# A hybrid decoder trunk on one core: the time-step weights as 64 columns side by side, and two row tiles' norm statistics moved to ScalarE

## The chip, the core and the metric

The kernel runs on one core of one Trainium2 chip. The core has five engines that matter here, each with an instruction stream of its own that runs in order: TensorE (PE in the profile, with its weight loads shown apart as PEld), VectorE (DVE), ScalarE (ACT), GpSimd (POOL) and SyncE (SP, which only issues DMAs). Semaphores tie the streams together. The metric is the device time of one execution in microseconds (us), given as the median of a few runs. TensorE was granted its full clock throughout (0.998 of it over the execution that was profiled).

## What is computed

The input is a residual stream `x` of 1024 positions by 1024 channels, in float32. It is normalised row by row, and then one layer follows: a wide projection whose columns feed a Conformer convolution branch and a Mamba-2 state-space branch, their gated sum, a second norm, and a causal convolution FFN with a third norm. Cut to what the change touches:

```python
def layer_norm(x, g, b):
    mu = jnp.mean(xf, axis=-1, keepdims=True)
    var = jnp.mean(jnp.square(xf - mu), axis=-1, keepdims=True)
    return (xf - mu) * lax.rsqrt(var + LN_EPS) * g + b
...
h = layer_norm(x, ln_in_g, ln_in_b)
u = h @ w_in[l]          # ... | ssm x,B,C | ssm dt (32 columns) | ...
...
dt = jax.nn.softplus(dt_raw + dt_bias)     # time steps, one for each of 32 heads
a_head = -jnp.exp(a_log)
```

The 32 columns `dt_raw` of the projection give the time steps, one for each position and head. They set the decays of the state-space branch.

## The kernel before, in words

**Precision.** A projection keeps float32 accuracy by splitting both factors in two parts, a rounded high part (`hi`, type fp32r) and the remainder (`lo`). Each product is then three matmuls: hi*hi, hi*lo and lo*hi (`mm3`, L164 to L169). For a weight tile of 128x1024 (eight blocks of 128x128, one for each group of 128 input channels), `weights` (L150) loads it into a buffer `st_...` by DMA, ScalarE copies the high part to `w_...` (L155), and VectorE, or GpSimd where it is told so, subtracts to get the low part (L156). There are three buffers for loads and three for split weights. A new weight tile's copy on ScalarE must wait until TensorE is done with the tile three before it.

**Halves.** The 1024 positions go in two halves of 512. A half has four row tiles of 128 positions. `ln_in` (L235) loads the four tiles `x_0` to `x_3`, normalises each, stores it for later, and transposes it by TensorE into `hT`, again as hi and lo.

**The input norm of a tile** (before): VectorE takes the statistics of two halves of the row (L208) and merges them to mean and variance (L222); ScalarE takes a square root (L223) and VectorE the reciprocal (L224); VectorE then applies it in two passes over the 128x1024 tile, in place: subtract the mean and multiply by the gain (L228), multiply by the reciprocal and add the bias (L231). TensorE transposes the tile in eight 128x128 blocks, four to a PSUM bank (L193); for each bank ScalarE copies the high part out (L199) and VectorE subtracts to get the low part (L200). There are four such PSUM banks (`sm_...`), so the banks of `x_2` are those that `x_0` used.

**The first columns** (`first_columns`, L349): three column tiles of the projection come first in each half, the time-step tile `w_c_40` (32 real columns, filled up with zeros to 128), one tile of B (`w_c_32`) and one of C (`w_c_36`). Each is multiplied with `hT` in two steps of 256 positions, so that the first step needs only `x_0` and `x_1`: for each tile and step, 3 products times 8 blocks = 24 matmuls of 128x256 (L358). That makes 144 matmuls a half. In the first half GpSimd subtracts the low parts of these three weight tiles, in the second VectorE does. After them come the columns of x, in matmuls of 128x512 (L167 to L169).

**The time steps** (`time_steps`, L262): ScalarE adds the bias to the 32 rows of the finished `dt` product (L265, `dtc`), TensorE transposes it in four pieces of 32x128 (L270), and a chain of small VectorE and ScalarE operations follows.

**What sets the order.** The program is written in loops, and a scheduler that plays through a timeline of its own orders the instructions of each engine, with the priorities given in the code (`tc.high_priority`). The order of each engine is fixed when the kernel is built. `x_0` and `x_1` have a higher priority than `x_2` and `x_3`. On TensorE the matmuls of the first columns and the transposes of `x_2` and `x_3` are woven into one another.

## Time and profile before

| | us |
|---|---|
| median of 3 runs | 2008.04 (2006.31 to 2008.36) |
| the execution that was profiled | 2007.04 |
| its span, first instruction to last | 2005.2 |
| TensorE busy in the span | 1971.1 (98%), 9164 matmul records |
| VectorE busy | 1693.9 (84%) |
| ScalarE busy | 1022.5 (51%) |
| GpSimd busy | 178.0 (9%) |

A timeline row gives the start, the length of the group, the engine, the line, the operation, output and inputs, shape, and how many instructions the group holds; square brackets name the idle time ahead of it and what ended it. Instructions on one engine overlap a little at their ends, and a matmul's shown length includes its way through the array, so distances between starts are what count there. In a row of the windows, each engine has its busy time and, in brackets, the number of its instructions in the window. In a group that is asked for by its line, three numbers give the shortest, the median and the longest duration in ns. The row of waits names who waited for what, the total, how often, and the longest.

### The profile page before, as it was taken

What the parts mean: (1) busy time and instruction counts of PE and PEld (TensorE: products, weight loads), DVE (VectorE), ACT (ScalarE), POOL (GpSimd) and SP (SyncE); (2) the same over time, 40 slices, a digit from 0 to 9 for tenths busy, and PEclk for the clock granted to TensorE, in tenths of its full rate; (3) what the DMA queues carried; (4) which work ended last, traced back from release to release, by engine and by line L of the source; (5) the groups of instructions that cost most, each with busy time, mean ns of one, the idle gap of its engine ahead of it and who ended that gap; (6) DMA issues with size and microseconds to landing.
All of it is one profiled execution on the core that took longest, in us unless ns stands there. A gap on an engine that the chain in (4) does not pass through costs nothing. (4 is left out here: it accounts for less than half of the span.)

```text
span 2005.2 us, 24594 instructions
## 1 busy us (share of the span) xinstructions
PE 1971.1 (98%) x9164; PEld 1620.4 (81%) x9164; DVE 1693.9 (84%) x2261; ACT 1022.5 (51%) x1480; POOL 178.0 (9%) x144
## 2 busy tenths in 40 slices
PE   7999999999999999999999999999999999999998
PEld 6888888888888888888888888877778888888886
DVE  7599999979865868999998977578998878778768
ACT  4465654556453265665545546255554444553432
POOL 2010101001300000100000122001000000011000
PEclk9999999999999999999999999999999999999999
DMA  6223223233445532222323253487442232368573
GB/s 222 88 70 95 79 87 123 85 111 106 168 128 183 221 109 74 84 90 85 115 90 111 100 173 121 131 283 250 146 158 104 100 121 95 106 217 266 184 241 110
DMA packets 97031, 272.20 MB, mean 136 GB/s; under 512 B 11216, under 2 KB 11216, under 8 KB 96912
## 3 DMA queue, kind: packets, MB, share of 16 engines
q1 hardware_dynamic: 88992, 246.78, 37.2%
q0 software_dynamic: 5616, 19.66, 2.7%
q10 hardware_dynamic: 2304, 4.20, 0.6%
q8 instruction: 72, 1.18, 0.3%
q14 instruction: 47, 0.39, 0.1%
HBM read 221.05 MB, written 49.55 MB: 135 GB/s over the span
## 5 line engine op out<-in xcount | busy, mean ns | idle before, releaser
L421 DVE SCALAR_TENSOR_TENSOR c<-v,pc,c 128x512 f32<-128x512 f32 x480 | 374.5, 803 | 6.4 <-ACT c L410 5.0
L479 POOL TENSOR_TENSOR au<-seg_mv,head_of 128x1024 fp32r<-128x1024 f32 x32 | 77.0, 2408 | 958.5 <-PE sm L488 728.2
L167 PE MATMUL acc<-hT,w_c 128*128 128x512 f32 x352 | 141.1, 401 | 0.0
L168 PE MATMUL acc<-hT,w_c 128*128 128x512 f32 x352 | 140.7, 400 | 0.0
L169 PE MATMUL acc<-hT,w_c 128*128 128x512 f32 x352 | 138.5, 393 | 0.0
L910 DVE SCALAR_TENSOR_TENSOR fo<-u,pc,fo 128x1024 f32<-128x1024 f32 x88 | 111.4, 1285 | 0.4 <-ACT fo L906 0.4
L376 DVE SCALAR_TENSOR_TENSOR xbc<-u,pc,xbc 128x512 f32<-128x512 f32 x144 | 109.6, 773 | 0.7 <-ACT xbc L374 0.5
L167 PE MATMUL acc<-h1s,w_s 128*128 128x512 f32 x264 | 104.5, 396 | 2.3 <-ACT u L894 2.3
L169 PE MATMUL acc<-h1s,w_s 128*128 128x512 f32 x264 | 104.0, 394 | 0.0
L168 PE MATMUL acc<-h1s,w_s 128*128 128x512 f32 x264 | 103.5, 392 | 0.0
L167 PE MATMUL acc<-w_z,hT 128*128 128x512 f32 x256 | 100.9, 401 | 0.0
L168 PE MATMUL acc<-w_z,hT 128*128 128x512 f32 x256 | 100.9, 394 | 0.0
L169 PE MATMUL acc<-w_z,hT 128*128 128x512 f32 x256 | 100.7, 396 | 0.0
L155 ACT CAST w_c<-st_c 128x1024 fp32r<-128x1024 f32 x50 | 52.6, 1052 | 88.9 <-PE acc L169 68.1
L1049 ACT CAST w_dn<-dr 128x1024 fp32r<-128x1024 f32 (+1 forms) x73 | 60.8, 842 | 71.9 <-DVE dr L979 31.1
L1050 DVE TENSOR_TENSOR w_dn<-dr,w_dn 128x1024 fp32r<-128x1024 f32 (+1 forms) x73 | 70.1, 967 | 14.8 <-ACT w_dn L1049 14.6
L168 PEld LDWEIGHTS acc<-hT,w_c 128*128 128x128 f32 x352 | 66.1, 188 | 17.0 <-issue 3.8
L169 PEld LDWEIGHTS acc<-hT,w_c 128*128 128x128 f32 x352 | 66.1, 188 | 16.2 <-issue 2.6
L167 PEld LDWEIGHTS acc<-hT,w_c 128*128 128x128 f32 x352 | 66.1, 188 | 16.0 <-issue 2.6
L156 DVE TENSOR_TENSOR w_c<-st_c,w_c 128x1024 fp32r<-128x1024 f32 x47 | 60.5, 1288 | 20.2 <-ACT w_c L155 20.2
L167 PE MATMUL sm<-h1b,w_s 128*128 128x512 f32 x176 | 69.6, 396 | 0.0
L169 PE MATMUL sm<-h1b,w_s 128*128 128x512 f32 x176 | 69.3, 394 | 0.0
(354 smaller groups left out, 5703.1 us busy)
## 6 DMA issues: line engine op xcount, KB each, us to landing
st_c<-wcol SPq DMA_DIRECT2D x50, 512.0 KB, 3.5
st_z<-wz SPq DMA_DIRECT2D x32, 512.0 KB, 3.5
st_wo<-wo SPq DMA_DIRECT2D x24, 512.0 KB, 4.0
ra<-wup SPq DMA_DIRECT2D x22, 512.0 KB, 3.5
rb<-wup SPq DMA_DIRECT2D x22, 512.0 KB, 3.4
t_scr<-fo POOLq DMA_DIRECT2D x22, 512.0 KB, 3.4
dr<-t_scr SPq DMA_DIRECT2D x44, 256.0 KB, 4.0
dr<-wdown SPq DMA_DIRECT2D x38, 256.0 KB, 4.3
```

Of the source, the lines that this page charges most:

```text
L155: A.copy(w[:, 0, :], st)
L156: (eng or V).tensor_tensor(out=w[:, 1, :], in0=st, in1=w[:, 0, :].bitcast(F32), op=ALU.subtract)
L167: TE.matmul(ps, wa(0), xa(0), start=start, stop=False, skip_group_check=more)
L168: TE.matmul(ps, wa(0), xa(1), start=False, stop=False, skip_group_check=more)
L169: TE.matmul(ps, wa(1), xa(0), start=False, stop=stop, skip_group_check=more)
L376: V.scalar_tensor_tensor(out=o, in0=u[:, k : k + HALF], scalar=pc[:, wc + k : wc + k + 1], in1=o, op0=ALU.mult, op1=ALU.add,)
L421: V.scalar_tensor_tensor(out=accs[i], in0=v[:, k : k + HALF], scalar=pc[:, wc + k : wc + k + 1], in1=accs[i], op0=ALU.mult, op1=ALU.add,)
L479: G.tensor_tensor(out=au, in0=seg_mv[:, c, :].unsqueeze(1).to_broadcast([P, 8, P]), in1=head_of[:, g, :].unsqueeze(2).to_broadcast([P, 8, P]),
L910: V.scalar_tensor_tensor(out=o, in0=u[:, k : k + T], scalar=pc[:, wc + k : wc + k + 1], in1=o, op0=ALU.mult, op1=ALU.add,)
L1049: A.copy(w[:, 0, cs], src)
L1050: V.tensor_tensor(out=w[:, 1, cs], in0=src, in1=w[:, 0, cs].bitcast(F32), op=ALU.subtract)
```

## The change

It has two parts.

**The time-step weights.** The tile of 128 columns, of which 32 are real, is replaced by 64 columns for each block: the 32 high parts and, beside them, the 32 low parts (`weights_side_by_side`). Only the real columns are split, 128x256 elements in place of 128x1024, by ScalarE and VectorE in both halves of the positions (GpSimd has no part in it any more). One matmul with these 64 columns gives hi*h and lo*h at once, in 64 rows of the output. With the high and the low part of `hT` that is 2 x 8 = 16 matmuls of 64x256 for each step of 256 positions in place of 24. The bias is added to 64 rows (it is zero in the second 32), and the four transposes become four float32 matmuls with a 64x32 matrix `fold`, two identities on top of each other, which add the two groups of rows while they transpose. (The product then holds lo*lo as well.)

**The statistics.** For `x_2` and `x_3` of the first half alone, `ln_stats_act` takes the place of the VectorE statistics: ScalarE passes over the tile once to sum it, multiplies the sum by -1/1024, passes over it a second time to sum the squares of what is left after the mean, and takes the square root with the factor 1/1024. VectorE still takes the reciprocal and applies the norm. The second pass reads the tile that VectorE's first step then overwrites.

```diff
+    fold = statep.tile([2 * HEADS, HEADS], F32, name="fold")
+    V.tensor_add(fold, ident[: 2 * HEADS, :HEADS], ident[: 2 * HEADS, HEADS : 2 * HEADS])
...
+    def weights_side_by_side(src, name):
+        with tc.high_priority(offset=4000):
+            st = wst.tile([P, D], F32, tag="st", name=f"st_{name}")
+            SY.dma_start(st, src)
+            w = wsp.tile([P, 2, D], F32R, tag="w", name=f"w_{name}")
+            sv = st.rearrange("p (k c) -> p k c", k=KD)[:, :, :HEADS]
+            wv = w[:, 0, : KD * 2 * HEADS].rearrange("p (k c) -> p k c", k=KD)
+            hi, lo = wv[:, :, :HEADS], wv[:, :, HEADS:]
+            A.copy(hi, sv)
+            V.tensor_tensor(out=lo, in0=sv, in1=hi.bitcast(F32), op=ALU.subtract)
+        return wv
...
+    def ln_stats_act(pl, t, name):
+        work = pl.tile([P, D], F32, tag="ln_work", name=f"work_{name}")
+        mv = pl.tile([P, 1, 2], F32, tag="ln_mv", bufs=2, name=f"mv_{name}")
+        rs = pl.tile([P, 1], F32, tag="ln_rs", bufs=2, name=f"rs_{name}")
+        mean, var = mv[:, 0, 0:1], mv[:, 0, 1:2]
+        A.activation(out=work, in_=t, func=AF.Identity, accum_out=var)
+        A.mul(mean, var, -1.0 / D)
+        A.activation(out=work, in_=t, func=AF.Square, bias=mean, accum_out=var)
+        A.activation(out=rs, in_=var, func=AF.Sqrt, bias=eps, scale=1.0 / D)
+        V.reciprocal(out=rs, in_=rs)
+        return mv, rs
...
-                    mv, rs = ln_stats(pl, [xt], f"in{hh}_{t}")
-                    ln_apply(xt, mv, rs, 0, *gb)
+                    if first and t >= 2:
+                        mv, rs = ln_stats_act(pl, xt, f"in{hh}_{t}")
+                        ln_apply(xt, mv, rs, 0, *gb, op=ALU.add)
+                    else:
+                        mv, rs = ln_stats(pl, [xt], f"in{hh}_{t}")
+                        ln_apply(xt, mv, rs, 0, *gb)
...
-        dtc = pl.tile([HEADS, HALF], F32, tag="yo", name=f"dtc{hh}")
+        n2 = 2 * HEADS
+        dtc = pl.tile([n2, HALF], F32, tag="yo", name=f"dtc{hh}")
...
-            TE.transpose(
+            TE.matmul(
                 pt[:, c * HEADS : (c + 1) * HEADS],
                 dtc[:, c * P : (c + 1) * P],
-                ident[:HEADS, :HEADS],
+                fold,
+                start=True,
+                stop=True,
             )
...
-        ws = [weights(wcol[ct], f"c{hh}_{ct}", eng=None if hh else G) for ct in cts]
+        wd = weights_side_by_side(wcol[cts[0]], f"c{hh}_{cts[0]}")
+        ws = [weights(wcol[ct], f"c{hh}_{ct}", eng=None if hh else G) for ct in cts[1:]]
         pss = [bank(1) for _ in cts]
         for q in range(2):
             ts = slice(q * 256, (q + 1) * 256)
-            for w, ps in zip(ws, pss):
+            for j in range(2):
+                for k in range(KD):
+                    TE.matmul(
+                        pss[0][: 2 * HEADS, ts],
+                        wd[:, k, :],
+                        hT[:, j, k, ts],
+                        start=j == 0 and k == 0,
+                        stop=j == 1 and k == KD - 1,
+                    )
+            for w, ps in zip(ws, pss[1:]):
```

The scheduler orders the engines anew. A row of an order gives the line, the operation, output and inputs, the shape, and how many such instructions follow each other. The line numbers of the changed kernel are higher: its transposes stand at L207, the time-step matmuls at L392, those of the other two tiles at L402, the matmuls with `fold` at L302, ScalarE's copies of the transposes at L213, of the weights at L157 and L171, and the x columns at L181 to L183.

TensorE in the first half, before, from the last transposes of `x_1` to those of `x_2` (`acc_322` is the time-step product, `acc_323` that of B, `acc_324` that of C):

```order
L193 MATMUL sm_249<-ident,x_1_193 128x128 x4
L358 MATMUL acc_322<-hT_187,w_c_40_309 128x256 x4
L358 MATMUL acc_323<-hT_187,w_c_32_314 128x256 x4
...
L358 MATMUL acc_322<-hT_187,w_c_40_309 128x256 x12
L358 MATMUL acc_324<-hT_187,w_c_36_319 128x256 x8
L358 MATMUL acc_323<-hT_187,w_c_32_314 128x256 x12
L358 MATMUL acc_322<-hT_187,w_c_40_309 128x256 x4
L358 MATMUL acc_323<-hT_187,w_c_32_314 128x256 x4
L193 MATMUL sm_267<-ident,x_2_199 128x128 x4
L193 MATMUL sm_274<-ident,x_2_199 128x128 x4
```

The same place now, from `x_1` to the last transposes of `x_3` (`acc_324` is now the time-step product, `acc_325` B, `acc_326` C):

```order
L207 MATMUL sm_251<-ident,x_1_195 128x128 x4
L207 MATMUL sm_269<-ident,x_2_201 128x128 x4
L207 MATMUL sm_276<-ident,x_2_201 128x128 x4
L392 MATMUL acc_324<-hT_189,w_c_40_311 64x256 x4
L402 MATMUL acc_325<-hT_189,w_c_32_316 128x256 x4
L392 MATMUL acc_324<-hT_189,w_c_40_311 64x256 x4
L402 MATMUL acc_325<-hT_189,w_c_32_316 128x256 x4
L392 MATMUL acc_324<-hT_189,w_c_40_311 64x256 x8
L402 MATMUL acc_325<-hT_189,w_c_32_316 128x256 x16
L402 MATMUL acc_326<-hT_189,w_c_36_321 128x256 x24
L207 MATMUL sm_294<-ident,x_3_203 128x128 x4
L207 MATMUL sm_301<-ident,x_3_203 128x128 x4
```

The transposes of `x_2` have moved ahead of all matmuls of the first columns; before, 56 of these stood between `x_1` and `x_2`, 14 more between `x_2` and `x_3`, and 74 behind `x_3`. Now 64 stand between `x_2` and `x_3`, and 64 behind `x_3`. There the time-step matmuls come in four groups of four, each with matmuls of 128 columns ahead of it and behind it, so that the time-step product is visited seven times in the first half.

ScalarE in the first half, before, from the copies of `x_0` on:

```order
L199 CAST hT_187<-sm_217 128x4x128
L199 CAST hT_187<-sm_224 128x4x128
L155 CAST w_c_40_309<-st_c_40_307 128x1024
L199 CAST hT_187<-sm_242 128x4x128
L155 CAST w_c_32_314<-st_c_32_312 128x1024
L199 CAST hT_187<-sm_249 128x4x128
L223 ACTIVATE rs_in_2_257<-mv_in_2_256,eps 128x1
L155 CAST w_c_36_319<-st_c_36_317 128x1024
L223 ACTIVATE rs_in_3_282<-mv_in_3_281,eps 128x1
```

And now (`work_in` is scratch, `mv_in` holds mean and sum of squares, `sm_219` and `sm_226` are the two banks of `x_0`, `sm_244` the first of `x_1`):

```order
L247 ACTIVATE work_in_2_258,mv_in_2_259<-x_2_201 128x1024
L248 ACTIVATE mv_in_2_259<-mv_in_2_259 128x1
L249 ACTIVATE work_in_2_258,mv_in_2_259<-x_2_201,mv_in_2_259 128x1024
L213 CAST hT_189<-sm_219 128x4x128
L247 ACTIVATE work_in_3_283,mv_in_3_284<-x_3_203 128x1024
L250 ACTIVATE rs_in_2_260<-mv_in_2_259,eps 128x1
L213 CAST hT_189<-sm_226 128x4x128
L171 CAST w_c_40_311<-st_c_40_309 128x8x32
L213 CAST hT_189<-sm_244 128x4x128
L248 ACTIVATE mv_in_3_284<-mv_in_3_284 128x1
L157 CAST w_c_32_316<-st_c_32_314 128x1024
```

Both passes over `x_2` stand ahead of the first copy of `x_0`, the first pass over `x_3` stands between the two copies of `x_0` and ahead of the square root for `x_2`, and the second pass over `x_3` follows behind the copies of `x_1`, just ahead of the copy of `w_c_36`. On VectorE, `x_2` is now applied straight after `x_1` (its second step between the two subtractions of `x_0`), the low part of the time-step weights stands ahead of the subtractions of `x_1`, and `x_3` is applied around the subtractions of `x_2`. GpSimd has `w_c_32` and `w_c_36` left.

TensorE in the second half, before:

```order
L358 MATMUL acc_5586<-hT_5146,w_c_40_5573 128x256 x24
L358 MATMUL acc_5587<-hT_5146,w_c_32_5578 128x256 x24
L358 MATMUL acc_5588<-hT_5146,w_c_36_5583 128x256 x8
L358 MATMUL acc_5586<-hT_5146,w_c_40_5573 128x256 x16
L358 MATMUL acc_5588<-hT_5146,w_c_36_5583 128x256 x16
L358 MATMUL acc_5586<-hT_5146,w_c_40_5573 128x256 x8
L358 MATMUL acc_5587<-hT_5146,w_c_32_5578 128x256 x24
L358 MATMUL acc_5588<-hT_5146,w_c_36_5583 128x256 x24
```

And now:

```order
L392 MATMUL acc_5572<-hT_5132,w_c_40_5559 64x256 x16
L402 MATMUL acc_5573<-hT_5132,w_c_32_5564 128x256 x24
L402 MATMUL acc_5574<-hT_5132,w_c_36_5569 128x256 x8
L392 MATMUL acc_5572<-hT_5132,w_c_40_5559 64x256 x16
L402 MATMUL acc_5573<-hT_5132,w_c_32_5564 128x256 x8
L402 MATMUL acc_5574<-hT_5132,w_c_36_5569 128x256 x16
L402 MATMUL acc_5573<-hT_5132,w_c_32_5564 128x256 x16
L402 MATMUL acc_5574<-hT_5132,w_c_36_5569 128x256 x24
```

16 matmuls are gone, and the time-step product is visited twice. Elsewhere the orders differ in a few places only, where small operations of the time steps and weight splits of the second half change places; the decay matmuls of the second half (L312 and L339) stand 21 rows later.

More of the change, by code (lines that the diff above doesn't have):

```diff
@@ L225, in ln_stats, with ln_apply @@
         return mv, rs
-    def ln_apply(t, mv, rs, i, g, b):
+    def ln_stats_act(pl, t, name):
[9 more added lines that the diff above has]
+        return mv, rs
+    def ln_apply(t, mv, rs, i, g, b, op=ALU.subtract):
         V.scalar_tensor_tensor(
-            out=t, in0=t, scalar=mv[:, i, 0:1], in1=g, op0=ALU.subtract, op1=ALU.mult
+            out=t, in0=t, scalar=mv[:, i, 0:1], in1=g, op0=op, op1=ALU.mult
         )
@@ L262, in time_steps @@
     def time_steps(pl, hh, ps):
-        dtc = pl.tile([HEADS, HALF], F32, tag="yo", name=f"dtc{hh}")
+        n2 = 2 * HEADS
+        dtc = pl.tile([n2, HALF], F32, tag="yo", name=f"dtc{hh}")
         A.activation(
-            out=dtc, in_=ps[:HEADS, :], func=AF.Identity, bias=pc[:HEADS, PC_DTB : PC_DTB + 1]
+            out=dtc, in_=ps[:n2, :], func=AF.Identity, bias=pc[:n2, PC_DTB : PC_DTB + 1]
         )
```

## The prediction

> **What bounds the kernel now.** I read the page's totals first, then the busy time by stretches, then who waited for whom on TensorE, and last the timeline of the two places that the change touches. Two lines of the page:
>
> ```profile
> PE 1971.1 (98%) x9164; PEld 1620.4 (81%) x9164; DVE 1693.9 (84%) x2261; ACT 1022.5 (51%) x1480; POOL 178.0 (9%) x144
> PEclk9999999999999999999999999999999999999999
> ```
>
> TensorE is busy for 98% of the span at full clock, so a gain has to be one of two things: fewer or shorter matmuls, or less of the 34 us (2005.2 - 1971.1) in which it waits. The windows show where those lie:
>
> ```profile
> 0.00:40.00 40.00, 25.01 (x184) 23.53 (x185) 29.23 (x46) 14.98 (x30) 10.86 (x15) 1.00 0.68 239
> 40.00:100.00 60.00, 60.00 (x275) 49.90 (x274) 35.84 (x61) 31.87 (x55) 3.43 (x1) 1.00 0.31 98
> 100.00:400.00 300.00, 300.00 (x1442) 245.82 (x1441) 298.71 (x410) 174.41 (x291) 28.60 (x12) 1.00 0.28 90
> 680.00:740.00 60.00, 60.00 (x343) 52.56 (x342) 48.59 (x84) 31.53 (x56) 0.42 (x1) 1.00 0.37 127
> ```
>
> 15 of the 34 us are in the first 40, before the first half's matmuls run without a gap. From 40 to 400 TensorE never waits, and it never waits from 680 to 740, where the second half's first columns lie. So time won at the head moves everything behind it forward, and a matmul saved in the second half counts in full. VectorE is as good as full from 100 to 400, but from 40 to 100 it idles for 24 us waiting for products, so it starts earlier too. The waits name the head's cause:
>
> ```profile
> PE sm L193 <- DVE x L231: 14.8, 3, 12.2
> ```
>
> TensorE waits for VectorE's second step of the norm. The timeline of the head, VectorE, ScalarE and GpSimd first:
>
> ```profile
> 8.30 2.48 DVE L228 SCALAR_TENSOR_TENSOR x<-x,mv_in,in_g 128x1024 f32<-128x1024 f32 x2 [1.04 <-DMA in_g<-prow]
> 10.77 2.46 DVE L231 SCALAR_TENSOR_TENSOR x<-x,rs_in,in_b 128x1024 f32<-128x1024 f32 x2
> 13.15 2.46 DVE L208 BATCH_NORM_STATS2 st_in<-x 128x6 f32<-128x512 f32 x4
> 13.30 0.59 ACT L199 CAST hT<-sm 128x512 fp32r<-128x512 f32 x1 [5.72 <-PE sm L193]
> 15.53 0.67 DVE L200 TENSOR_TENSOR hT<-sm,hT 128x512 fp32r<-128x512 f32 x1
> 15.77 9.05 POOL L156 TENSOR_TENSOR w_c<-st_c,w_c 128x1024 fp32r<-128x1024 f32 x3 [13.33 <-ACT w_c L155]
> 16.07 1.06 ACT L155 CAST w_c<-st_c 128x1024 fp32r<-128x1024 f32 x1
> 17.46 5.12 DVE L228 SCALAR_TENSOR_TENSOR x<-x,mv_in,in_g 128x1024 f32<-128x1024 f32 x2
> 17.49 0.31 ACT L223 ACTIVATE rs_in<-mv_in,eps 128x1 f32<-128x1 f32 x1
> 23.29 3.82 DVE L231 SCALAR_TENSOR_TENSOR x<-x,rs_in,in_b 128x1024 f32<-128x1024 f32 x2
> ```
>
> One norm step takes 1.24 us (2.48 / 2) for `x_0` and `x_1`, but 2.56 and 1.91 for `x_2` and `x_3`, with GpSimd at work beside them. GpSimd's own three subtractions vary as well:
>
> ```profile
> L156 POOL TENSOR_TENSOR w_c<-st_c,w_c x3: 2391/3369/3377, 15.8 to 21.5; 128x1024 fp32r<-128x1024 f32 x3
> ```
>
> 3.37 is 2.39 plus about one norm step. So the two take turns, each holding the other up for a whole instruction. Now TensorE:
>
> ```profile
> 26.05 1.07 PE L193 MATMUL sm<-ident,x 128*128 128x128 f32 x8 [1.60 <-DVE x L231]
> 28.64 1.03 PE L193 MATMUL sm<-ident,x 128*128 128x128 f32 x8
> 29.43 9.38 PE L358 MATMUL acc<-hT,w_c 128*128 128x256 f32 x74
> 29.91 8.69 PEld L358 LDWEIGHTS acc<-hT,w_c 128*128 128x128 f32 x72 [0.21 <-ACT hT L199]
> 38.29 0.52 PE L358 MATMUL acc<-hT,w_c 128*128 128x256 f32 x3
> 38.74 0.43 PE L270 MATMUL sm<-ident,dtc 32*128 32x32 f32 x4
> 39.10 0.50 PE L167 MATMUL acc<-hT,w_c 128*128 128x512 f32 x1
> 39.43 0.40 PE L168 MATMUL acc<-hT,w_c 128*128 128x512 f32 x1
> ```
>
> From 26.05, where `x_2` arrives, TensorE has work almost without a gap. 88 of the 144 first-column matmuls are still to come there, and they end at about 38.65.
>
> **The first half's chain, step by step.** The second pair of tiles lands late, and their DMAs are not touched:
>
> ```profile
> 2.67 0.94 SPq L244 DMA_DIRECT2D x<-x  x2
> x<-x SPq DMA_DIRECT2D x1, 512.0 KB, 8.1
> ```
>
> `x_2` is issued at 2.67 and lands 8.1 later, at 10.8. ScalarE is idle then (its row at 13.30 shows 5.72 us of it). What an accumulating pass costs shows in the one that the kernel has, over 512 elements:
>
> ```profile
> L539 ACT ACTIVATE sq<-t x32: 613/632/657, 130.5 to 1168.2; 128x512 f32<-128x512 f32 x32
> L539 ACT ACTIVATION_READ_ACCUMULATOR sq<-t x32: 183/187/222, 131.0 to 1168.7; 128x1 f32 x32
> ```
>
> Such a pass is two instructions. Over 1024 elements I take 1.06 (the copy at 16.07) plus 0.19, so 1.25, as the nearest; twice 0.63 would give 1.45. Two passes with a 0.25 multiplication between them (bounds: nothing, and the square root's 0.31) end at 13.5. VectorE is done with `x_1` at 13.2, so it waits 0.3. First step of `x_2`: 14.75. One subtraction of `x_0` (0.67): 15.4. ScalarE's square root for `x_2` stands behind the copy of `x_0` (0.59) and the first pass over `x_3` (1.25), and ends at 15.6. With the reciprocal and the second step, `x_2` is ready at 17.0, against 26.0 before. Of these 9 us, 2.46 are the four statistics, the rest is order, and the turns with GpSimd, which now starts only after the second step.
>
> TensorE transposes `x_2` (0.9, with a short wait for `x_0`'s bank). The low part of the time-step weights holds it to about 18.1: another 0.67 and then a subtraction of 256 elements, which I put at 0.4, between nothing and the 0.67 of 512. From there TensorE itself is the bound. Its step for a matmul of 256 columns is read from the second half:
>
> ```profile
> 685.77 17.44 PE L358 MATMUL acc<-hT,w_c 128*128 128x256 f32 x144
> 703.05 0.40 PE L167 MATMUL acc<-hT,w_c 128*128 128x512 f32 x1
> 703.28 0.40 PE L168 MATMUL acc<-hT,w_c 128*128 128x512 f32 x1
> ```
>
> (703.05 - 685.77) / 144 = 0.12 us. I take the same for 64 columns as for 128, since the moving side is 256 long in both. 64 matmuls, 7.7 us, end at 25.9; the transposes of `x_3` take 0.8; the copy out of the first bank makes the next matmul start 1.27 after the transposes began (29.91 - 28.64); 64 more take 7.7, and a restart 0.1. The end is at 35.0, against 38.65: a gain of 3.65.
>
> Does `x_3` hold this up? ScalarE's second pass over it ends at about 19.9 (from 15.6: five copies and a multiplication make 3.0, the pass 1.25). VectorE's first step then waits for GpSimd's subtraction of `w_c_32` (18.2 to 20.6) and ends at 21.85; the second waits for that of `w_c_36` (to 24.25) and ends at 25.5. TensorE wants it at 25.9. The cover is 0.4 us, and if it goes, each further 0.1 costs 0.1.
>
> The matmuls with `fold`: a float32 matmul counts as two records here (the decay matmuls below, 8 in the code, 16 records), so eight pieces in place of four transposes.
>
> ```profile
> L312 PE MATMUL sm<-upper,sp_ax x16: 270/275/275, 65.5 to 734.9; 128*128 128x128 f32 x16
> L270 PE MATMUL sm<-ident,dtc x8: 221/222/243, 38.7 to 708.8; 32*128 32x32 f32 x8
> ```
>
> The four transposes start (0.43 - 0.22) / 3 = 0.07 apart, so four more pieces are 0.25 to 0.3: -0.25. First half so far: 3.4.
>
> **The price of changing the tile.** All matmuls but these transposes run as 128*128; they run as 32*128. Around them, from the last 128x256 matmul (38.29 + 2 x 0.12 = 38.53) to L168 at 39.43 there are 0.90 us. Without them it would be 0.12 + 0.23 = 0.35, and the four themselves are 0.28, so going into another tile shape and back costs 0.27. The time-step matmuls are a 128*64 tile, for which no row exists. The bounds are nothing, if only the row side matters, and 0.27 or somewhat more a visit; I take 0.27, from the one change of shape that the trace has. Nine visits (seven and two) cost 1.9 + 0.55. The Trainium skill, TensorEngine Tiling (Array Packing), section Tiling Modes, says that changing the tiling mode, and not just the tile, drains TensorE, and counts 128x64 among the modes. By that rule a price is due at each visit; by a reading of the row as something of row tiles alone, none. The sum by the one is 2.6, by the other 5.0.
>
> **The second half.** 16 matmuls less, 1.9 us, -0.25 for `fold`, -0.55 for two visits: 1.1. The split of `w_c_40` shrinks on ScalarE and VectorE (1.05 and 1.2 before), off TensorE's path. The x weights that come next wait for the buffers of `w_c_40`, which TensorE now leaves earlier. The decay matmuls stand 21 rows later, about 5 us, and their results are used only some 30 us after.
>
> **The sum.** 3.4 - 1.9 + 1.9 - 0.25 - 0.55 = 2.6 us. On the profiled execution (2007.04, of which 2005.2 are span) that makes 2004.4; the median of the runs is 1.0 above that execution, so the forecast is 2008.04 - 2.6 = 2005.4. What else gets earlier is covered by TensorE's own queue: the weights of x are copied at the pace at which TensorE frees buffers.
>
> **Rivals.**
>
> *No price for the tile.* The 128*64 tile only masks columns. For it: nothing in the trace shows a column change costing; against: the 0.27 above. Then the nine visits are free, and 2.6 + 9 x 0.27 = 5.0 us are won: 2003.0.
>
> *The weight loads come into the open (slower).* Every matmul has its own load, hidden behind the matmul before it. In a short matmul the load shows:
>
> ```profile
> L535 PE MATMUL sm<-xs,m 128*128 128x64 f32 x512 | 60.5, 271 | 0.0
> ```
>
> 60.5 / 512 = 0.12 for matmuls of 64 moving columns, as long as one of 256. If a 128*64 tile could not load beside its running matmul, each of the 64 would be 0.24: +7.7, so 5.1 slower, 2013.1. It decides from 0.04 a matmul. Against it: the transposes in their 32*128 tile start 0.07 apart, below even that load.
>
> *ScalarE is late.* `x_2` now heads TensorE's stream, and three accumulating passes stand ahead of its readiness. If a pass is 1.6 or more, or VectorE and GpSimd take turns the other way round for `x_3`, 1 to 2.5 us of the first half are lost: 2006.4 to 2007.9.
>
> **How the numbers follow.** Forecast 0.52, no price 0.28, late ScalarE 0.13, open loads 0.07. A measurement of this kernel can tell about 0.2%, 4.0 us, from no change; so faster means below 2004.0. The case without a price mostly gets there (0.26 of its 0.28), the forecast with a tail (0.06): 0.32. Slower is most of the last rival: 0.06. The rest is 0.62. The range goes from 2002.0 (no price, 1.0 for unknown sizes) to 2008.6 (late ScalarE with nothing won, 0.5 for the spread of runs); it leaves out the open loads and tails.
>
> **What would show it.** In the changed profile: `x_2`'s transposes at about 17.0 and 64 matmuls without a gap behind them; `x_3`'s transposes at 25.9 to 26.9; the first x matmul at about 37 (35 if the tile is free); at each change between 64 and 128 columns a start 0.1 to 0.2 late; 64-column matmuls 0.12 apart; in the second half 128 matmuls in about 15.9 us. I am wrong if these matmuls are farther apart, if TensorE waits long for ScalarE or VectorE after 18, or if new waits behind 40 give time back.

## The result, and the profile after it

The changed kernel takes 2002.33 us (median of 18 runs, 2000.20 to 2004.43), the kernel before beside it 2006.17 us (18 runs, 2004.09 to 2009.67). The ratio is 0.9978 with a 95% interval of 0.9972 to 0.9985: 4.4 us faster, 3.0 to 5.6 (the two medians alone are 3.8 apart). The forecast was 2.6 us faster, with a change of less than 0.2% the likeliest; the rival without a price for the tile had said 5.0. The change is 0.22% faster, 0.15 to 0.28: clear of no change, and just above the line of 0.2% that the prediction drew. The forecast of 2005.4 started from three runs of the kernel before with a median of 2008.04; over 18 runs it is 1.9 lower, and that part of the distance from 2005.4 to 2002.33 has nothing to do with the change.

The profiled execution has a span of 1999.0 us (2005.2 before). From the windows of the changed kernel:

```profile
0.00:40.00 40.00, 26.02 (x187) 24.42 (x188) 27.93 (x48) 22.53 (x47) 7.46 (x14) 1.00 0.72 254
680.00:740.00 60.00, 60.00 (x337) 52.32 (x336) 47.97 (x83) 31.15 (x56) 2.20 (x1) 1.00 0.41 137
```

TensorE is busy 1 us longer in the first 40, and has 16 matmuls, 1.9 us, less to do there; from 680 to 740 it still never waits. The head of the timeline, VectorE, ScalarE and GpSimd together:

```profile
11.01 1.06 ACT L247 ACTIVATE work_in<-x 128x1024 f32<-128x1024 f32 x1 [3.41 <-DVE rs_in L238]
11.97 0.19 ACT L247 ACTIVATION_READ_ACCUMULATOR work_in<-x 128x1 f32 x1
12.43 1.15 ACT L249 ACTIVATE work_in<-x,mv_in 128x1024 f32<-128x1024 f32 x1
...
15.69 1.28 DVE L258 SCALAR_TENSOR_TENSOR x<-x,rs_in,in_b 128x1024 f32<-128x1024 f32 x1
17.49 0.42 DVE L172 TENSOR_TENSOR w_c<-st_c,w_c 128x256 fp32r<-128x256 f32 x1
17.75 5.77 POOL L158 TENSOR_TENSOR w_c<-st_c,w_c 128x1024 fp32r<-128x1024 f32 x2 [15.28 <-ACT w_c L157]
22.56 2.05 DVE L258 SCALAR_TENSOR_TENSOR x<-x,rs_in,in_b 128x1024 f32<-128x1024 f32 x1
```

`x_2` is ready at 17.0 and `x_3` at 24.6; forecast were 17.0 and 25.5. TensorE in the same stretch:

```profile
17.12 1.17 PE L207 MATMUL sm<-ident,x 128*128 128x128 f32 x8 [1.47 <-DVE x L258]
18.06 0.70 PE L392 MATMUL acc<-hT,w_c 128*64 128x256 f32 x4
18.59 0.63 PE L402 MATMUL acc<-hT,w_c 128*128 128x256 f32 x4
19.07 0.62 PE L392 MATMUL acc<-hT,w_c 128*64 128x256 f32 x4
25.72 1.03 PE L207 MATMUL sm<-ident,x 128*128 128x128 f32 x8
26.99 0.68 PE L392 MATMUL acc<-hT,w_c 128*64 128x256 f32 x4 [0.24 <-ACT hT L213]
34.64 0.40 PE L181 MATMUL acc<-hT,w_c 128*128 128x512 f32 x1
34.88 0.40 PE L182 MATMUL acc<-hT,w_c 128*128 128x512 f32 x1
35.20 1.07 PE L302 MATMUL sm<-fold,dtc 64*128 64x32 f32 x8
...
36.54 0.39 PE L181 MATMUL acc<-hT,w_c 128*128 128x512 f32 x1
```

The tile changes from 64 to 128 columns at 18.59 and back at 19.07. Four matmuls and a change take 0.53 (the first four, with the start) and 0.48: 0.12 a matmul, no more than without a change. Around the four matmuls with `fold` it is otherwise: from 34.88 to 36.54 there are 1.66 us, two x matmuls of 0.23 among them, so 1.20 for them; before, the four transposes took 0.56 (1.02 from L169 at 708.29 to L168 at 709.31 in the second half, less 0.46). To compare the first halves I take the start of the fourth x matmul, behind the time-step pieces in both: 39.90 before, 36.54 now, 3.35 us before rounding. These rows of the kernel before:

```profile
39.90 0.39 PE L167 MATMUL acc<-hT,w_c 128*128 128x512 f32 x1
...
708.29 0.39 PE L169 MATMUL acc<-hT,w_c 128*128 128x512 f32 x1
...
709.31 0.40 PE L168 MATMUL acc<-hT,w_c 128*128 128x512 f32 x1
```

The second half of the changed kernel:

```profile
682.81 1.99 PE L392 MATMUL acc<-hT,w_c 128*64 128x256 f32 x16
684.63 4.00 PE L402 MATMUL acc<-hT,w_c 128*128 128x256 f32 x32
688.47 1.99 PE L392 MATMUL acc<-hT,w_c 128*64 128x256 f32 x16
...
697.97 0.40 PE L181 MATMUL acc<-hT,w_c 128*128 128x512 f32 x1
...
703.21 0.39 PE L183 MATMUL acc<-hT,w_c 128*128 128x512 f32 x1
703.53 1.07 PE L302 MATMUL sm<-fold,dtc 64*128 64x32 f32 x8
...
704.87 0.39 PE L182 MATMUL acc<-hT,w_c 128*128 128x512 f32 x1
```

128 matmuls take 697.97 - 682.81 = 15.16, against 17.28 for 144 (703.05 - 685.77): 2.12 won. Those of 64 columns are (684.63 - 682.81) / 16 = 0.114 apart, those of 128 (688.47 - 684.63) / 32 = 0.12. The fold matmuls take 1.66 - 0.46 = 1.20 again, 0.64 more than the transposes. So this half wins 1.48, and both together 4.83, inside the measured 3.0 to 5.6. The rest of the 6.2 us between the two spans comes and goes at waits far from the change (last section).

### The profile page after: what moved, and what is told of

The parts are those of the page before. It is cut to its first block, busy times and chain, and to the rows that moved or that the text cites. A ratio compares the mean times of both kernels' runs of the same rounds, so it can differ in the third digit from the quotient of the medians.

```text
span 1999.0 us, 24559 instructions
## 1 busy us (share of the span) xinstructions
PE 1966.9 (98%) x9140; PEld 1617.5 (81%) x9140; DVE 1688.6 (84%) x2257; ACT 1026.0 (51%) x1490; POOL 171.8 (9%) x143
## 4 chain that ended last, share of the span: by engine, by line
PE 85%; DVE 10%; issue 2%; DMA 2%; ACT 1%; SPq 0%; DVEq 0%; ACTq 0%
PE acc L181 22%; PE acc L183 22%; PE acc L182 22%; DVE c L465 3%; PE sm L181 3%; PE sm L183 3%; PE sm L182 3%; PE sm L579 2%; PE acc L402 1%; PE sm L560 1%; PE sm L568 1%; PE sm L207 1%; PE sm L532 1%; PE sm L517 1%; DVE rows L255 0%
## 5 line engine op out<-in xcount | busy, mean ns | idle before, releaser
L181 PE MATMUL acc<-hT,w_c 128*128 128x512 f32 x352 | 140.9, 400 | 0.0
L183 PE MATMUL acc<-hT,w_c 128*128 128x512 f32 x352 | 138.6, 394 | 0.0
L181 PE MATMUL acc<-h1s,w_s 128*128 128x512 f32 x264 | 104.5, 396 | 2.3 <-ACT u L938 2.3
L183 PE MATMUL acc<-h1s,w_s 128*128 128x512 f32 x264 | 104.0, 394 | 0.0
L181 PE MATMUL acc<-w_z,hT 128*128 128x512 f32 x256 | 100.8, 401 | 0.0
L183 PE MATMUL acc<-w_z,hT 128*128 128x512 f32 x256 | 100.7, 396 | 0.0
L157 ACT CAST w_c<-st_c 128x1024 fp32r<-128x1024 f32 x48 | 50.4, 1051 | 88.6 <-PE acc L183 66.1
L183 PEld LDWEIGHTS acc<-hT,w_c 128*128 128x128 f32 x352 | 66.1, 188 | 16.1 <-issue 2.6
L181 PEld LDWEIGHTS acc<-hT,w_c 128*128 128x128 f32 x352 | 66.1, 188 | 15.9 <-issue 2.6
L181 PE MATMUL sm<-h1b,w_s 128*128 128x512 f32 x176 | 69.6, 396 | 0.0
L183 PE MATMUL sm<-h1b,w_s 128*128 128x512 f32 x176 | 69.3, 394 | 0.0
```

What stands on the lines that cost most here:

```text
L157: A.copy(w[:, 0, :], st)
L181: TE.matmul(ps, wa(0), xa(0), start=start, stop=False, skip_group_check=more)
L183: TE.matmul(ps, wa(1), xa(0), start=False, stop=stop, skip_group_check=more)
```

## The experiments

The theory after the result: the two columns of the time-step matmuls change for nothing, the fold matmuls cost 0.64 a half more than the transposes, and the rest went as forecast. Its first rival: the change of tile does cost 0.27 a visit, and something unseen gave 2.4 us back. A second theory came up with the first four runs, on TensorE's rate at the start. Each ratio is to runs of the kernel before beside it on the same chip; the last column comes from a single execution.

| kernel | median us (runs) | ratio to before, 95% interval | fourth x matmul of its profile |
|---|---|---|---|
| before | 2006.17 (18) | 1 | 39.90 |
| changed | 2002.33 (18) | 0.9978 (0.9972 to 0.9985) | 36.54 |
| weights_only | 2005.93 (11) | 0.9995 (0.9987 to 1.0004) | 40.26 |
| stats_only | 2005.74 (11) | 0.9995 (0.9986 to 1.0004) | 40.00 |
| pad128 | 2002.41 (11) | 0.9979 (0.9970 to 0.9988) | 38.55 |
| interleaved | 2001.93 (10) | 0.9978 (0.9968 to 0.9987) | 36.30 |
| transposes | 1998.35 (5) | 0.9958 (0.9946 to 0.9971) | 35.68 |
| fold128 | 2001.54 (1) | (single run) | 37.64 |
| after_warm | 2001.20 (7) | 0.9974 (0.9963 to 0.9985) | 37.89 |
| before_warm | 2005.33 (11) | 0.9995 (0.9986 to 1.0004) | 41.79 |
| transposes_warm | 2001.30 (7) | 0.9975 (0.9964 to 0.9986) | 38.21 |
| kept_after | 2001.34 (6) | 0.9970 (0.9958 to 0.9982) | 36.83 |
| kept_before | 2005.88 (11) | 0.9996 (0.9987 to 1.0004) | 41.09 |
| kept_transposes | 2000.18 (5) | 0.9964 (0.9951 to 0.9976) | 36.68 |
| kept_stats | 2005.11 (11) | 0.9993 (0.9984 to 1.0002) | 39.15 |
| kept_stats_weights_v | 2000.80 (7) | 0.9972 (0.9961 to 0.9982) | 37.83 |

### Does a change of columns cost? (pad128, interleaved)

`pad128`: the stationary side is 128 wide and reads on into the next 64 columns, so no matmul changes the column tile; rows 64 to 127 of the result are not used.

```diff
+            A.copy(w[:, 0, KD * 2 * HEADS : (KD + 1) * 2 * HEADS], st[:, : 2 * HEADS])
...
-                        pss[0][: 2 * HEADS, ts],
-                        wd[:, k, :],
+                        pss[0][:, ts],
+                        wd[:, 0, k * 2 * HEADS : k * 2 * HEADS + P],
```

> The changed kernel with the time-step matmuls 128 columns wide (the next 64 columns stand behind them, and their products are not used), so that no matmul changes the column tile; the number of matmuls is the same. Theory (the change of columns is free): no gain; first x matmul at 34.6 to 35.2, the second half's 128 matmuls in 15.2 to 15.5 us, the time 0 to 0.7 us above that of the changed kernel. Rival (0.27 a visit, nine visits): 2.4 us faster than the changed kernel, first x matmul at 32.8.

Over all runs it equals the changed kernel (0.9979 against 0.9978), and its second half takes 15.35 us for the 128 matmuls (15.16). Had it saved 2.4 us, the ratio would be 0.9966, outside its interval of 0.9970 to 0.9988. But the profile does not fit the first half expected: the first x matmul at 36.66, 1.5 to 2 us late. The reason is in the runs on the rate, below.

`interleaved`: in the second half each time-step matmul stands ahead of one of `w_c_32`.

```diff
+            if not hh:
+                for jk in range(2 * KD):
+                    time_step(jk)
...
+                        if hh and not m and n < 2:
+                            time_step(n * KD + k)
```

> The changed kernel with the second half's time-step matmuls put between those of the next weights one by one, so that TensorE goes to 64 columns and back some 20 times there instead of twice. Theory (a change of columns is free): the second half's 128 first-column matmuls take 15.2 us as in the changed kernel, and the time is the changed kernel's within 0.7 us. Rival (0.27 us a visit): 18 visits more, so 4.9 us more: 20 us for the 128 matmuls, and 2007 us.

TensorE goes to 64 columns 21 times here, 2 times in the changed kernel. Its timeline, the first of these changes and the end of the first columns:

```profile
682.75 1.53 PE L393 MATMUL acc<-hT,w_c 128*64 128x256 f32 x12
...
685.55 0.28 PE L393 MATMUL acc<-hT,w_c 128*64 128x256 f32 x1
685.67 0.28 PE L409 MATMUL acc<-hT,w_c 128*128 128x256 f32 x1
685.78 0.28 PE L393 MATMUL acc<-hT,w_c 128*64 128x256 f32 x1
...
697.88 0.40 PE L181 MATMUL acc<-hT,w_c 128*128 128x512 f32 x1
```

The starts are 0.11 to 0.12 apart through the changes, and the 128 matmuls take 15.13 us. 19 visits more at 0.27 would be 5.1 us. The change of columns is free, to some 0.005 us a change; this rival has fallen.

### What do the fold matmuls cost? (fold128, transposes)

`fold128`, built on `pad128`, has `dtc` and `fold` on 128 rows, so that they change no row tile:

```diff
-    fold = statep.tile([2 * HEADS, HEADS], F32, name="fold")
+    fold = statep.tile([P, HEADS], F32, name="fold")
...
-        n2 = 2 * HEADS
+        n2 = P
```

`transposes` transposes 64 rows and lets VectorE add the halves:

```diff
-            TE.matmul(
-                pt[:, c * HEADS : (c + 1) * HEADS],
-                dtc[:, c * P : (c + 1) * P],
-                fold,
-                start=True,
-                stop=True,
+            TE.transpose(
+                pt[:, c * n2 : (c + 1) * n2], dtc[:, c * P : (c + 1) * P], ident[:n2, :n2]
             )
...
-        V.tensor_copy(v, pt[:, :n])
...
+        V.tensor_copy(vv, pv[:, :, 0, :])
+        V.tensor_tensor(out=vv, in0=vv, in1=pv[:, :, 1, :], op=ALU.add)
```

> The version with 128 columns throughout, with the fold matmuls over 128 rows as well (the rows below the first 64 of fold are zero), so that no matmul changes the tile in rows either. From the end of the matmul before the fold matmuls to the start of the one behind them the changed kernel takes 1.66 us with two x matmuls of 0.23 in it, so 1.2 us. Theory (a change of rows costs 0.2 to 0.3 us, the rest is eight records 0.11 apart): 0.9 us here. Rival (a change of rows is free as well): 1.2 us.

> The changed kernel with four transposes of 64 x 128 in place of the four matmuls with fold, and VectorE adding the two halves (one copy and one addition in place of one copy). Theory (the fold matmuls cost 1.2 us of TensorE a half, because each is two records 0.11 apart): four records at 0.07 to 0.11, so 0.55 to 0.65 of TensorE a half; 1.2 us faster than the changed kernel in all. Rival (the price is the change of rows, not the records): the same 1.2 a half, no gain.

The timeline of `fold128` around them, then that of `transposes`:

```profile
36.28 0.40 PE L183 MATMUL acc<-hT,w_c 128*128 128x512 f32 x1
36.51 0.98 PE L303 MATMUL sm<-fold,dtc 128*128 128x32 f32 x8
37.33 0.48 PE L184 MATMUL acc<-hT,w_c 128*128 128x512 f32 x1
37.64 0.39 PE L182 MATMUL acc<-hT,w_c 128*128 128x512 f32 x1
```

```profile
34.63 0.40 PE L180 MATMUL acc<-hT,w_c 128*128 128x512 f32 x1
34.96 0.46 PE L300 MATMUL sm<-ident,dtc 64*128 64x64 f32 x4
35.35 0.50 PE L181 MATMUL acc<-hT,w_c 128*128 128x512 f32 x1
35.68 0.39 PE L179 MATMUL acc<-hT,w_c 128*128 128x512 f32 x1
```

In `fold128` the stretch is 37.64 - 36.28 - 0.46 = 0.90, as the theory said: eight records take 0.82, and going in and out of the 64-row tile costs the other 0.30. The start behind L183 shows it: 0.23 there, 0.32 (34.88 to 35.20) with 64 rows. In `transposes` it is 35.68 - 34.63 - 0.46 = 0.59, and 0.58 in the second half: 0.61 less than the fold matmuls in each half, 1.2 in all. That settles the cost on TensorE. The time went further: 8.4 us below before (5.8 to 10.8), with only 5 runs. The 4.4 of the change and 1.2 make 5.6, just below that interval; the versions with transposes below come to 5.0 and 7.2. So a gain over the changed kernel of about 1.2 is shown on TensorE; the further 2.8 of that one set of runs are not explained.

### Each part alone (weights_only, stats_only)

```diff
-                    if first and t >= 2:
+                    if first and t >= 4:
```

This is `weights_only`: all statistics stay on VectorE. `stats_only` has the weights, the first columns and the transposes of the kernel before, and keeps `ln_stats_act`.

> The weights side by side alone; all four row tiles have their statistics from VectorE as before. Theory (a change between 128 and 64 columns is free, the fold matmuls cost 0.65 us a half more than the transposes): the second half has after's numbers, 128 matmuls in 15.2 us, and wins 2.1 - 0.65 = 1.5 us. In the first half x_2 and x_3 stay behind VectorE and GpSimd, so x_3 decides: its transposes at 27 to 28.6, then 1.27 and 64 x 0.117, so the first x matmul at 36 to 37.5, against 39.1 before, less 0.65. In all 2.4 to 4 us faster than before. Rival (0.27 us for each visit to 64 columns): 2 us less, so 0.4 to 2 us faster.

> ScalarE's statistics for x_2 and x_3 alone; the time-step weights as before, three matmuls a step with 128 columns, their low part by GpSimd. Theory: x_2's transposes come at 17 as in the changed kernel, but GpSimd now has three subtractions in a row for TensorE to wait for, the last ending at 25 to 26, and 144 matmuls take 17.3 us: first x matmul at 37 to 38, a gain of 1 to 2 us, and nothing in the second half. If the statistics carry the whole change: 3.4 us faster or more, with the first x matmul at 35.5.

Both are 1.0 us faster than before by the middle of their intervals (-0.8 to 2.6 and -0.8 to 2.8), which neither tells from no change; each falls short of the 3.0 to 5.6 of the whole. `weights_only` gets the second half's gain (128 matmuls in 15.16 us), but its fourth x matmul is 0.4 later than before, not 1 to 2.5 us earlier. Two rows of its timeline show what holds the head up:

```profile
17.01 2.47 DVE L172 TENSOR_TENSOR w_c<-st_c,w_c 128x256 fp32r<-128x256 f32 x1
19.62 1.94 PE L392 MATMUL acc<-hT,w_c 128*64 128x256 f32 x8 [3.77 <-DVE w_c L172]
```

The short subtraction, 0.42 in the changed kernel, stood up for a whole subtraction of GpSimd (16.84 to 19.19), TensorE was idle for 3.8 us, and then its matmuls were 0.22 apart ((21.36 - 19.62) / 8), at a granted clock of 0.50 from 18.9 to 22.4. The matmuls with the weights side by side need the low part from the first on; in the kernel before, TensorE began at 16.23 with the high part alone. So here it is not `x_3` that binds, as the expectation had it: `x_3` is ready at 27.1, and TensorE comes to it only at 28.45, busy without a gap from 19.62. At full clock it would have come there at about 27.1 as well (an estimate: 1.4 of the 2.7 us at half rate taken off), so `x_3`, which the changed kernel has ready at 24.6, would be the next bound. In `stats_only` `x_2` comes at 17.44 as expected, but the fourth x matmul at 40.00, with TensorE at half rate for a part (next section). What the two profiles show is that each part alone leaves a bound standing: without the short time-step weights TensorE has 144 matmuls and GpSimd three subtractions; without the statistics `x_3` comes at 27.1. That the two win more together than the sum of their single gains lies in the profiles, and is not clear of the noise in the times.

### TensorE's rate at the start (after_warm, before_warm, transposes_warm)

`pad128` and `stats_only` were late for another reason too. From the timeline of `pad128`, from the transposes of `x_2` on:

```profile
17.53 1.94 PE L208 MATMUL sm<-ident,x 128*128 128x128 f32 x8 [1.22 <-DVE x L259]
19.12 1.20 PE L393 MATMUL acc<-hT,w_c 128*128 128x256 f32 x4
20.12 0.92 PE L403 MATMUL acc<-hT,w_c 128*128 128x256 f32 x4
```

Eight transposes of `x_2` take 1.6 us from the first to the next start (0.94 in the changed kernel, 17.12 to 18.06), and the matmuls behind them are 0.25 apart instead of 0.12: TensorE works at half rate until about 20.8. The granted clock reads 1.00 there; in this trace it shows no half rate before the first change. The changed kernel's own profile had full rate from 15 on. So its 3.35 us hold a start that another execution does not get (the profile of the kernel before had full rate from 15 on too).

The first try to take this out: 28 idle matmuls of the constant `ones` on TensorE from 1.3 us on, in three kernels.

```diff
+    with tc.high_priority(offset=8000):
+        idle = bank(0)
+        for _ in range(28):
+            TE.matmul(idle[:, :P], ones, ones, start=True, stop=True)
```

> The changed kernel with 28 idle matmuls of the constant ones on TensorE from about 1.3 us on, while it has nothing else to do; their products are not used. Theory (TensorE starts at half rate and goes to full rate only about 3 us of work later, at a point that shifts from one execution to another, and the changed kernel pays for it when that point comes after 17 us): x_0's transposes are 0.11 apart rather than 0.24, the time-step matmuls 0.12 apart from the first on, first x matmul at 34.4 to 34.7; the median is 0.5 to 2 us below the changed kernel's and the runs lie closer together. Rival (the difference between the profiles is one of transfers, not of TensorE's rate): the same median as the changed kernel within 0.5 us.

> The kernel before with the same 28 idle matmuls. Theory: there TensorE waits for GpSimd at 21.5 and for x_2 at 26 anyway, so a slow start is hidden: first x matmul at 38.5 to 39.1, and a median 0 to 0.8 us below before's. If the rate at the start costs the kernel before as much as the changed one, it gains 1 to 2 us too, and the start has no part in the difference between the two.

> The version with four transposes of 64 rows in place of the fold matmuls, with the 28 idle matmuls at the start. Theory: 1.2 us below the changed kernel with idle matmuls, so 1998 to 2000 us, 6 to 8 us below the kernel before; the 8 us that the transposes alone showed hold 1 to 2 us of lucky starts. Rival: the transposes themselves win 4 us, and this version comes to 1997 or less.

It failed, and showed more than a success would have. The idle matmuls end at 9.56, and TensorE is idle until 12.0 and again for 1.96 us up to 17.48. The windows of `after_warm` (TensorE's busy time, granted clock, transfers):

```profile
10.00:12.00 2.00, 0.00 (x0) 0.96 1.03 420
12.00:14.00 2.00, 2.00 (x10) 0.50 1.02 418
14.00:16.00 2.00, 1.52 (x8) 0.68 0.98 365
16.00:18.00 2.00, 0.52 (x5) 1.00 0.85 338
18.00:20.00 2.00, 2.00 (x15) 0.67 1.02 365
20.00:22.00 2.00, 2.00 (x12) 0.50 0.79 252
22.00:24.00 2.00, 2.00 (x18) 0.98 0.71 264
```

In these traces the clock is 1 or 0.5, so a mean of 0.68 is 1.28 us of half rate. The changes lie at 11.84, 15.28, 18.68 and 22.08: 3.44, 3.40 and 3.40 apart, while TensorE's own work began at 12.00, 17.48 and 18.33. So the rate is decided on a grid of 3.4 us that the kernel does not set: a stretch that was idle for the most part brings half rate for the next one, a busy one full rate. The Trainium skill says this, in TensorE: Matmul & The Clock Gate, section Part 1: The HAM clock gate: a free-running window of 3.4 us, half rate by default, full rate after a busy window. The runs agree with it, in the length and in that the kernel's start does not set it.

The profile of `transposes_warm` was at half rate from 11.7 to 21.9, and over its 7 runs it was no faster than `after_warm` (2001.30 and 2001.20), where 1.2 us had been expected; that the half rate took them is likely, but not shown. `before_warm` came to 0.9995 (0.9986 to 1.0004), and its fourth x matmul was 1.9 later. 0.8 of that is `x_0`, which came at 13.0 rather than 12.2; that moves by 1 us between these profiles with the landing of the norm's two rows. The rest arises at VectorE beside GpSimd: its second steps for `x_2` and `x_3` took 4.51 us in place of 3.82.

### TensorE kept busy (kept_after, kept_before, kept_transposes, kept_stats)

34 idle matmuls at the start, and 7 more behind the transposes of `x_1`:

```diff
                     transpose_to(hT, xt, t, 0, KD)
+                    if first and t == 1:
+                        idle_matmuls(7)
```

> The changed kernel with TensorE kept busy up to the arrival of x_2: 34 idle matmuls of the constant ones from 1.3 us on, and 7 more behind the transposes of x_1, so that no stretch of 3.4 us before 18 us is less than about half busy. Theory (the rate is decided at the ends of stretches of 3.4 us on a grid that the kernel does not set; a busy stretch brings full rate, an idle one half): full rate from 17 to the end in every execution, x_2's transposes and the first matmuls 0.11 to 0.12 apart, first x matmul at 34 to 34.7, a median 0.5 to 1.5 us below the changed kernel's, so 2000.5 to 2001.8, and no slow start in the profile. Rival (the rate after 17 us does not matter to the end): the changed kernel's median within 0.3 us.

> The kernel before with the same 41 idle matmuls. Theory: x_2 and x_3 come from VectorE at 26 and 28.6 whatever TensorE's rate was until then, so the first x matmul stays at 38.5 to 39.5 and the median within 0.7 us of before's. Rival (a slow start costs the kernel before as much): 1 to 2 us faster.

> Four transposes of 64 rows in place of the fold matmuls, and TensorE kept busy as above. Theory: 1.2 us below the changed kernel kept busy, 1999 to 2000.5 us, 6 to 7 us below the kernel before. Rival (in the long run the transposes win nothing, and the 1998.35 was luck): the same as the changed kernel kept busy.

> ScalarE's statistics alone, time-step weights as before, and TensorE kept busy up to x_2 by the 41 idle matmuls. Theory (the statistics alone had TensorE at half rate until 21.3 in their profile, which took 1.6 us of what they win): first columns from 18.2 at full rate, 72 x 0.12, 1.27, 72 x 0.12, so the first x matmul at 37 to 37.7 instead of 39.2, and a median 1 to 2 us below the kernel before. Rival (without the shorter time-step weights the statistics win nothing, because GpSimd's three subtractions hold the first columns up): first x matmul at 39 again, no gain.

> The changed kernel kept busy once more, beside the one above on the same chip, to have the two compared there. Theory: 2 to 4 us faster than the statistics alone kept busy (16 matmuls fewer and cheaper in each half, 1.9 - 0.65 us and 2.1 - 0.65 us). Rival: within 1 us of each other.

In `kept_after` (run twice, the second time as `kept_stats_weights_v`) all is at full rate from 17.5 on, as expected, but the fourth x matmul is at 36.83 and 37.83, not earlier than the changed kernel's good start: `x_2` comes 0.4 later, because in the new order the second copy and the second subtraction of `x_0` stand ahead of its second step, and in the second profile `x_0` came at 13.0. The times, 6.0 us (3.6 to 8.4) and 5.6 us (3.6 to 7.8) below before, cannot be told from the changed kernel's 4.4. So the half rate is shown in the profiles, at about 1.5 us where it falls on the first columns; that it costs the changed kernel something on the average is not shown.

`kept_transposes` is 7.2 us (4.8 to 9.8) below before, 1.2 below `kept_after` on the same chip: the size expected, within the spread.

`kept_before` went against its theory: the fourth x matmul is 1.2 later than in the kernel before. TensorE waited 2.06 us for `x_2` up to 25.95, and its windows show what follows:

```profile
24.00:26.00 2.00, 0.05 (x1) 0.99 0.01 4
26.00:28.00 2.00, 2.00 (x10) 0.50 0.74 256
28.00:30.00 2.00, 2.00 (x14) 0.66 0.93 211
```

Half rate from 25.96 to 29.36, just when the transposes of `x_2` and `x_3` come. So the kernel before is not safe from it either: its long wait for `x_2` can bring the half rate itself (the wait of 1.60 in its own profile did not). The change takes that wait away.

`kept_stats` shows how much of `stats_only` was the rate: its fourth x matmul is at 39.15 instead of 40.00, 0.75 before that of the kernel before; 1.5 to 2 had been expected. Its time is 1.4 us (-0.4 to 3.2) below before, not clear of no change. The missing part:

```profile
17.63 8.19 POOL L163 TENSOR_TENSOR w_c<-st_c,w_c 128x1024 fp32r<-128x1024 f32 x3 [15.19 <-ACT w_c L162]
25.87 2.18 PE L384 MATMUL acc<-hT,w_c 128*128 128x256 f32 x16 [0.43 <-POOL w_c L163]
```

GpSimd's third subtraction ends at 25.8 and TensorE waits for it. That was the rival of this run, and it holds for a part: in this profile the statistics alone win only 0.75 us in the first half, with GpSimd and 16 more matmuls as the next bound. Against `kept_stats_weights_v` on the same chip the time differs by 4.3 us; 1.3 of that are the first half (39.15 to 37.83) and 1.5 the second; the rest lies within the spread of the runs.

## Why the prediction was wrong, point by point

- **`x_2` and ScalarE.** Right: the two passes took 1.15 and 1.24 to the end of their readings (1.25), `x_2` ready at 17.0, TensorE's first time-step matmul at 18.06 (18.1). The subtraction of 256 elements took 0.42 (0.4); it was done at 17.9 and held nothing up, for the matmul started straight behind the transposes.
- **`x_3`.** Ready at 24.6 (25.5); its transposes at 25.72 (25.9; the prediction's own 18.1 and 7.7 make 25.8), then 1.27 to the next matmul (1.27). The cover was 1.1 instead of 0.4. ScalarE was not late.
- **The price of changing the tile.** This is the step that failed: "I take 0.27, from the one change of shape that the trace has". That row was of a tile with fewer rows. A change of rows did cost 0.30 (`fold128` against the changed kernel); a change of columns costs nothing (`interleaved`, 21 visits). Nine visits at 0.27, 2.45 us, were to be struck out, and without them the sum is 5.0. The Trainium skill's rule (TensorEngine Tiling (Array Packing), section Tiling Modes) that a change of mode drains TensorE fits the 0.30 for the rows here, and not the columns, where the starts stay 0.11 to 0.12 apart through each change.
- **The matmuls with `fold`.** Too small: 0.25 a half was forecast, 0.64 measured. The eight records are 0.11 apart, not 0.07. The transposes' 0.07 was taken for a step that holds for any small matmul.
- **The 64 columns.** Taken as 0.12 apart, measured 0.114; 0.4 us in our favour over both halves.
- **The second half.** Forecast 1.1, measured 2.12 - 0.64 = 1.48: the two errors above, with 0.55 for two visits taken off.
- **The first half.** With the price 3.4 - 1.9 = 1.5, without it 3.4; measured 3.35. That the two agree so closely is luck: the first x matmul came 0.36 earlier than forecast (34.64 against 35.0), and the `fold` matmuls cost 0.39 more. It is also an execution in which TensorE reached full rate early. The forecast knew nothing of that rate: it read a full clock off the page's row of nines, as the first section does with its full clock throughout. In that same profile the transposes of `x_0` and `x_1` are 0.21 apart, against 0.11 for those of `x_2`:

```profile
12.18 3.34 PE L193 MATMUL sm<-ident,x 128*128 128x128 f32 x16 [12.18 <-DVE x L231]
```

- **The sum.** 3.35 + 1.48 = 4.8 by the profile, 4.4 by the runs. Without the price it is 5.0; `fold` takes 0.78 from it, the 64 columns add 0.4, and the first half's smaller terms 0.2. What turned up by mechanism is the rival "no price for the tile", given 0.28.

## What to carry to other kernels

A price read off one row holds for what that row changed: the only tile change in the trace was one of rows, and the new one was of columns. Where a term rests on such a likeness and decides the outcome, its two ends should be weighed by what differs physically, rows or columns, not by which row is nearest. And the parts of a change are to be judged together: here each alone left a bound standing that the other takes away, and neither could be told from no change.

## What else the runs showed of the hardware

- TensorE's rate goes between full and half on a grid of 3.4 us, and the changes of it in the first 30 us go with differences of up to 2 us in the fourth x matmul (36.54 in the changed kernel, 38.55 in `pad128`). How busy a stretch has to be can be read off these profiles: at half rate, one in which TensorE was busy for 80% (`weights_only`, 18.9 to 22.4) brought the full rate and one with 70% (`pad128`, 13.9 to 17.3) did not; at full rate, 57% (the changed kernel, 15.2 to 18.7) kept it and 43% (`after_warm`, 15.3 to 18.7) lost it.
- A float32 matmul with 32 moving columns is two records of 0.11 us; a transpose of 64 x 128 is one, 0.06 behind the transpose before it. Weights of 64 columns load in 0.134 us, those of 128 in 0.19, both hidden.
- One wait, which no part of the change touches, was in 12 of the 16 profiles: TensorE waits 0.5 to 1.1 us near 340 for VectorE's new state, in the stretch where VectorE is as good as full. It is in `kept_before` and `before_warm`, which are late there, and is missing in the kernel before, in `transposes`, `fold128` and one of the two profiles of `kept_after`'s program; so it belongs neither to the change nor to being early. In the changed kernel's profile it gives back 1.1 us of the head's gain, the sign of being wrong that the prediction had named, but the kernel before can have it too. Taken matmul by matmul, the lead of the one profile over the other is 3.3 us up to there, 2.2 behind it, 3.0 behind a shorter wait near 657, 4.5 behind the second half's first columns, 6.7 behind two waits near 1330 that are longer in the kernel before, 7.4 at 1405 and 6.2 at the end. So the 6.2 of the two spans is the 4.8 of the change and what these waits happened to be. What sets them was not tried.
